# A 64 KB write of zeros beside the first loads, on a batched matmul that keeps its DMA engines full

## Chip, cores and metric

One core of a Trainium2 chip. The time is the device time of one execution in microseconds (us). A program on one core has no second die to compare with, so the state of a run (fast or slow) is judged against the fastest run of the same kernel.

## The reference

```python
batch, m, k, n = 16, 512, 768, 1024
x: (batch, k, m) float32,  y: (batch, k, n) float32
out = np.einsum('bkm,bkn->bmn', x, y)      # (batch, m, n) float32
```

Each batch reads 1.57 MB of x and 3.15 MB of y and writes 2.10 MB: 109 MB in all.

## The kernel before

SyncE issues everything that moves: per batch the load of x, the load of y, and the store of the batch four back (`LAG`). VectorE casts both to bf16, PE multiplies, ScalarE copies the sums out of PSUM. The last four stores, that of the last batch among them, follow after the loop. In the views PE stands for TensorE's matmuls, PEld for its weight loads, DVE for VectorE, ACT for ScalarE and POOL for GpSimd.

```python
    LAG = 4
    o_tiles = {}

    def store(b):
        nc.sync.dma_start(o_v[b], o_tiles.pop(b)[:])

    with tc.manual_schedule():
        for b in range(B):
            xs = xs_pool.tile([P, KT, M], FP32, name="xs")      # 2 buffers
            ys = ys_pool.tile([P, KT, N], FP32, name="ys")      # 2 buffers
            nc.sync.dma_start(xs[:], x_v[b])
            nc.sync.dma_start(ys[:], y_v[b])
            if b >= LAG:
                store(b - LAG)
            # ... casts on VectorE, 48 matmuls, 8 copies on ScalarE into o_sb (5 buffers) ...
            o_tiles[b] = o_sb
        for b in sorted(o_tiles):
            store(b)
```

Of the kernel before, what the change touches and what calls it, by code (L numbers as in the profile page):

```python
# [1 line left out]

_os.environ.setdefault("NEURON_RT_ULTRASERVER_MODE", "4")

# [1 line left out]

# [4 lines left out]


@with_exitstack
def kernel(
    ctx: ExitStack,
    tc: tile.TileContext,
    x: bass.AP,
    y: bass.AP,
    out: bass.AP,
):  # L20
    nc = tc.nc
    P = 128
    FP32 = mybir.dt.float32
    BF16 = mybir.dt.bfloat16

    B, K, M = x.shape
    _, _, N = y.shape
    KT = K // P
    MT = M // P
    NF = 512  # L30
    NT = N // NF



    x_v = x.rearrange("b (p ko) m -> b p ko m", ko=KT)
    y_v = y.rearrange("b (p ko) n -> b p ko n", ko=KT)
    o_v = out.rearrange("b (p mo) n -> b p mo n", mo=MT)

    xs_pool = ctx.enter_context(tc.tile_pool(name="xs_pool", bufs=2))
    ys_pool = ctx.enter_context(tc.tile_pool(name="ys_pool", bufs=2))  # L40
    x_pool = ctx.enter_context(tc.tile_pool(name="x_pool", bufs=2))
    y_pool = ctx.enter_context(tc.tile_pool(name="y_pool", bufs=2))
    o_pool = ctx.enter_context(tc.tile_pool(name="o_pool", bufs=5))
    psum = ctx.enter_context(tc.tile_pool(name="psum", bufs=8, space=bass.MemoryType.PSUM))
    LAG = 4

    o_tiles = {}

    def store(b):
        nc.sync.dma_start(o_v[b], o_tiles.pop(b)[:])  # L50

    with tc.manual_schedule():
        for b in range(B):
            xs = xs_pool.tile([P, KT, M], FP32, name="xs")
            ys = ys_pool.tile([P, KT, N], FP32, name="ys")
            nc.sync.dma_start(xs[:], x_v[b])  # L56
            nc.sync.dma_start(ys[:], y_v[b])  # L57
            if b >= LAG:
                store(b - LAG)
            x_sb = x_pool.tile([P, KT, M], BF16, name="x_sb")  # L60
            y_sb = y_pool.tile([P, KT, N], BF16, name="y_sb")
            nc.vector.tensor_copy(x_sb[:], xs[:])  # L62
            for h in range(2):
                ks = slice(h * KT // 2, (h + 1) * KT // 2)
                nc.vector.tensor_copy(y_sb[:, ks], ys[:, ks])  # L65
            x_w = x_sb[:].rearrange("p k (j mo) -> p k mo j", mo=MT)
            o_sb = o_pool.tile([P, MT, N], FP32, name="o_sb")
            o_tiles[b] = o_sb
            for mo in range(MT):
                for nt in range(NT):  # L70
                    ns = slice(nt * NF, (nt + 1) * NF)
                    ps = psum.tile([P, NF], FP32, name="ps")
                    for kt in range(KT):
                        nc.tensor.matmul(ps[:], x_w[:, kt, mo], y_sb[:, kt, ns],  # L74
                                         start=(kt == 0), stop=(kt == KT - 1))
                    nc.scalar.copy(o_sb[:, mo, ns], ps[:])  # L76
            if False:
                store(b)
        for b in sorted(o_tiles):
            store(b)  # L80


# [1 line left out]
_INS = ['x', 'y']  # L84
_OUTS = [((16, 512, 1024), 'float32')]


# [23 lines left out]
```

## Time and profile before

| | before |
|---|---|
| median of 6 runs (lowest to highest) | 261.97 us (261.90 to 262.24) |
| bytes moved, mean rate | 109.18 MB, 420 GB/s |
| DMA engines busy in slices 1 to 38 (of 40, counted from 0) | 90% or more |
| PE, VectorE, ScalarE busy | 74%, 32%, 29% |
| last y landed, to the end of the span | 235.0 us, 25.0 us more |

Read it from the DMA row: every slice but the first and the last is full, so only bytes, or time that the DMA engines lose, can move the end. The lines for this are shown in the prediction below.

### The profile page before, as it was taken

The numbers are of one execution on the slowest core, as the hardware profiler recorded it, in microseconds if no ns is written. First come the engines' busy times: TensorE is split into PE (matmuls) and PEld (weight loads), VectorE is DVE, ScalarE is ACT, GpSimd is POOL, SyncE is SP. The second block draws the span as 40 slices with busy tenths as digits, with TensorE's granted clock in tenths as the row PEclk, the third lists the DMA queues.
The fourth block names the chain that finished last, engine by engine and source line by source line (L and its number), as shares of the span: only waits on it lengthen the run. The fifth ranks groups of instructions, "written<-read, shape, count | busy, mean of one in ns | idle before, by whom it ended". The sixth has DMA issues, their size and how long they took to land.

```text
span 260.1 us, 1877 instructions
## 1 busy us (share of the span) xinstructions
PE 192.3 (74%) x768; PEld 89.3 (34%) x768; DVE 83.0 (32%) x48; ACT 76.4 (29%) x129; POOL 0.2 (0%) x4
## 2 busy tenths in 40 slices
PE   0059999896947939599597886939779395895950
PEld 0014555353523514235143342514334142351420
DVE  0271643525213252222524215252132522225000
ACT  1003444342421403314123241413324042141330
POOL 0000000000000000000000000000000000000000
PEclk9999999999997998959779797997999899796895
DMA  7999999999999999999999999999999999999995
GB/s 299 427 423 420 438 433 427 431 369 422 430 430 432 432 430 435 430 432 423 433 435 421 438 422 438 429 427 437 435 424 424 432 431 430 437 425 432 431 408 242
DMA packets 6921, 109.18 MB, mean 420 GB/s; under 512 B 768, under 2 KB 768, under 8 KB 768
## 3 DMA queue, kind: packets, MB, share of 16 engines
q1 hardware_dynamic: 6912, 109.05, 98.5%
q8 instruction: 6, 0.10, 0.1%
q14 instruction: 3, 0.02, 0.0%
HBM read 75.50 MB, written 33.55 MB: 419 GB/s over the span
## 4 chain that ended last, share of the span: by engine, by line
DMA 80%; DVE 10%; PE 5%; DVEq 1%; SPq 0%; issue 0%; ACT 0%
DMA ys<-in_y_dram 80%; DVE y_sb L65 10%; PE ps L74 5%; DVEq L106 1%; SPq L56 0%; ACT o_sb L76 0%; SPq L57 0%; DVEq L65 0%
## 5 line engine op out<-in xcount | busy, mean ns | idle before, releaser
L74 PE MATMUL ps<-y_sb,x_sb 128*128 128x512 bf16 x768 | 192.3, 413 | 58.4 <-DVE y_sb L65 58.4
L74 PEld LDWEIGHTS <-x_sb 128*128 128x128 bf16 x768 | 89.3, 118 | 160.9 <-issue 47.5
L76 ACT COPY o_sb<-ps 128x512 f32<-128x512 f32 x128 | 75.2, 587 | 174.1 <-PE ps L74 174.1
L65 DVE CAST y_sb<-ys 128x3072 bf16<-128x3072 f32 x32 | 54.9, 1757 | 89.4 <-DMA ys<-in_y_dram 89.4
L62 DVE CAST x_sb<-xs 128x3072 bf16<-128x3072 f32 x16 | 28.2, 1760 | 66.2 <-DMA xs<-in_x_dram 55.2
L76 ACT ACT_TABLE_LOAD x1 | 1.3, 1283 | 0.7 <-PEq L95 0.7
L95 POOL MEMSET const-uint8-127<- 128x1 uint8 x1 | 0.1, 103 | 0.0
L95 POOL MEMSET const-bfloat16-1.0<- 128x1 bf16 x1 | 0.1, 102 | 0.0
L95 POOL MEMSET const-float32-1.0<- 128x1 f32 x1 | 0.1, 100 | 0.0
L95 POOL MEMSET const-float32-0.0<- 128x1 f32 x1 | 0.1, 99 | 0.2 <-issue 0.2
## 6 DMA issues: line engine op xcount, KB each, us to landing
ys<-in_y_dram SPq DMA_DIRECT2D x16, 3072.0 KB, 28.1
out_dram<-o_sb SPq DMA_DIRECT2D x16, 2048.0 KB, 32.6
xs<-in_x_dram SPq DMA_DIRECT2D x16, 1536.0 KB, 29.7
```

Source lines behind the costliest of these rows:

```text
L62: nc.vector.tensor_copy(x_sb[:], xs[:])
L65: nc.vector.tensor_copy(y_sb[:, ks], ys[:, ks])
L74: nc.tensor.matmul(ps[:], x_w[:, kt, mo], y_sb[:, kt, ns], start=(kt == 0), stop=(kt == KT - 1))
L76: nc.scalar.copy(o_sb[:, mo, ns], ps[:])
L95: nc = _bacc.Bacc("TRN2", target_bir_lowering=False, num_devices=1)
L106: with _tile.TileContext(nc) as tc:
```

## The change

The intent: write something early to the output, so that whatever a first write costs falls where the loads are only starting, and not into the full stream. The rest of the diff rewrites the loops for a number of halves that is 1 here; the instructions on every engine, but for the two new ones (a memset on VectorE, a DMA issue on ScalarE), stay the same in the same order.

```diff
+        z_pool = ctx.enter_context(tc.tile_pool(name="z_pool", bufs=1))
+        z = z_pool.tile([P, 128], FP32, name="z")
+        nc.vector.memset(z[:], 0.0)
+        nc.scalar.dma_start(o_v[B - 1, :, 0, 0:128], z[:])
+
         for b in range(B):
             xs = xs_pool.tile([P, KT, M], FP32, name="xs")
             ys = ys_pool.tile([P, KT, N], FP32, name="ys")
-            nc.sync.dma_start(xs[:], x_v[b])
-            nc.sync.dma_start(ys[:], y_v[b])
+            halves = 1
+
+            load(xs[:], x_v[b], 1)
+            # ... cut: load of y in one half, matmul loop over one half: same instructions, same order
```

More of the change, by code (lines that the diff above doesn't have):

```diff
@@ L45, with load, mm @@
     LAG = 4
+    KH = KT // 2
     o_tiles = {}
+    def load(dst, src, rows):
+        nc.sync.dma_start(dst, src)
     def store(b):
         nc.sync.dma_start(o_v[b], o_tiles.pop(b)[:])
+    def mm(ps, x_w, y_sb, kt, mo, nt):
+        nc.tensor.matmul(ps[:], x_w[:, kt, mo], y_sb[:, kt, nt * NF:(nt + 1) * NF],
+                         start=(kt == 0), stop=(kt == KT - 1))
     with tc.manual_schedule():
+        z_pool = ctx.enter_context(tc.tile_pool(name="z_pool", bufs=1))
+        z = z_pool.tile([P, 128], FP32, name="z")
+        nc.vector.memset(z[:], 0.0)
+        nc.scalar.dma_start(o_v[B - 1, :, 0, 0:128], z[:])
         for b in range(B):
@@ L55 @@
             ys = ys_pool.tile([P, KT, N], FP32, name="ys")
-            nc.sync.dma_start(xs[:], x_v[b])
-            nc.sync.dma_start(ys[:], y_v[b])
+            halves = 1
+            load(xs[:], x_v[b], 1)
+            for h in range(halves):
+                ks = slice(h * KT // halves, (h + 1) * KT // halves)
+                load(ys[:, ks], y_v[b, :, ks], 1)
             if b >= LAG:
@@ L63 @@
             for h in range(2):
-                ks = slice(h * KT // 2, (h + 1) * KT // 2)
+                ks = slice(h * KH, (h + 1) * KH)
                 nc.vector.tensor_copy(y_sb[:, ks], ys[:, ks])
@@ L68 @@
             o_tiles[b] = o_sb
-            for mo in range(MT):
-                for nt in range(NT):
-                    ns = slice(nt * NF, (nt + 1) * NF)
-                    ps = psum.tile([P, NF], FP32, name="ps")
-                    for kt in range(KT):
-                        nc.tensor.matmul(ps[:], x_w[:, kt, mo], y_sb[:, kt, ns],
-                                         start=(kt == 0), stop=(kt == KT - 1))
-                    nc.scalar.copy(o_sb[:, mo, ns], ps[:])
-            if False:
-                store(b)
+            ps = {}
+            for h in range(halves):
+                for mo in range(MT):
+                    for nt in range(NT):
+                        if h == 0:
+                            ps[mo, nt] = psum.tile([P, NF], FP32, name="ps")
+                        for kt in range(h * KT // halves, (h + 1) * KT // halves):
+                            mm(ps[mo, nt], x_w, y_sb, kt, mo, nt)
+                        if h == halves - 1:
+                            nc.scalar.copy(o_sb[:, mo, nt * NF:(nt + 1) * NF], ps[mo, nt][:])
         for b in sorted(o_tiles):
```

## The prediction

> **What bounds the kernel now.** I read the page first: the chain that ended last, then the slices, then the waits, then the stretches in which the slices dip.
>
> ```profile
> DMA ys<-in_y_dram 80%; DVE y_sb L65 10%; PE ps L74 5%; DVEq L106 1%; SPq L56 0%; ACT o_sb L76 0%; SPq L57 0%; DVEq L65 0%
> DMA  7999999999999999999999999999999999999995
> GB/s 299 427 423 420 438 433 427 431 369 422 430 430 432 432 430 435 430 432 423 433 435 421 438 422 438 429 427 437 435 424 424 432 431 430 437 425 432 431 408 242
> q1 hardware_dynamic: 6912, 109.05, 98.5%
> ```
>
> The reader is to see three things. The chain is 80% loads of y. The 16 DMA engines are at 90% or more in every slice but the first and the last, and one queue (q1, SyncE's) carries nearly all of it. PE has 74% and all other engines less than 35%. So the kernel moves 109 MB at about 430 GB/s; time changes if bytes change or if the engines lose time. In the slices I look for lost time: slice 0 (start), slice 8 (369 where its neighbours have 430), slices 38 and 39 (end).
>
> The y load takes 28.1 us from issue to landing in the page's table of issues, while 3 MB at 430 GB/s are 7.3 us. So four to five transfers stand in the queue at any moment: a transfer that is issued later or earlier by a microsecond changes nothing, and a microsecond lost by all DMA engines is lost at the end.
>
> Slice 8 covers 52.0 to 58.5 us. In single microseconds (stretch, busy time of PE, PEld, DVE, ACT, POOL, granted clock, DMA share, GB/s):
>
> ```profile
> 54.00:55.00 1.00, 1.00 (x7) 0.51 (x5) 0.00 (x0) 0.59 (x1) 0.00 (x0) 1.00 0.97 418
> 55.00:56.00 1.00, 1.00 (x6) 0.52 (x5) 0.00 (x0) 0.59 (x1) 0.00 (x0) 1.00 1.26 393
> 56.00:57.00 1.00, 1.00 (x6) 0.56 (x5) 0.00 (x0) 0.34 (x1) 0.00 (x0) 1.00 0.79 221
> 57.00:58.00 1.00, 1.00 (x7) 0.49 (x6) 0.00 (x0) 0.29 (x2) 0.00 (x0) 1.00 1.03 311
> 58.00:59.00 1.00, 1.00 (x6) 0.54 (x5) 0.00 (x0) 0.54 (x1) 0.00 (x0) 1.00 0.73 311
> 59.00:60.00 1.00, 1.00 (x6) 0.54 (x5) 0.00 (x0) 0.59 (x1) 0.00 (x0) 1.00 0.97 418
> ```
>
> From 55 to 59 us the core moved 1236 KB in place of 4 x 430 = 1720: 484 KB short, 1.1 us of the engines' time. No other stretch between 3 and 250 us dips like this. What happens there? In SyncE's part of the timeline, the first store of the program is issued behind the y load of batch 4:
>
> ```profile
> 39.71 0.33 SPq L57 DMA_DIRECT2D ys<-in_y_dram  x1
> 40.09 0.42 SPq L50 DMA_DIRECT2D out_dram<-o_sb  x1
> ```
>
> Ahead of it in the queue are five batches of loads, 5 x 4.72 MB = 23.6 MB, which at 425 GB/s are 55.5 us after the first packet at 1.7 us: the first store reaches the engines at about 57 us. The trace's packet records agree: its first packet starts at 57.74 us, and the last one or two y packets of each DMA engine before it took 1.3 to 1.96 us where a y packet takes 0.91. The excess, summed over 54 to 58 us and divided by 16, is 0.92 us per engine. The later stores show none: between 60 and 250 us the excess stays under 0.06 us in every 10 us. So the first write of the program, or the first on this queue, costs each engine 0.92 us, once, at the price of reads that stand ahead of it. That is what the change can act on.
>
> The end (same columns):
>
> ```profile
> 250.00:251.00 1.00, 0.67 (x4) 0.11 (x1) 0.00 (x0) 0.29 (x2) 0.00 (x0) 1.00 0.88 377
> 251.00:252.00 1.00, 0.00 (x0) 0.00 (x0) 0.00 (x0) 0.29 (x1) 0.00 (x0) 1.00 0.66 279
> 252.00:253.00 1.00, 0.00 (x0) 0.00 (x0) 0.00 (x0) 0.00 (x0) 0.00 (x0) 1.00 1.19 508
> ```
>
> The last y lands at 235.0 us, batch 15's matmuls and copies end at 251.3, and its store follows. The engines have by then nearly drained stores 11 to 14 (four times 2.1 MB, 19.5 us at 430): only around 251.5 us are some of them free. Both paths start from the landing of the last y, so a saving or a loss before it moves the whole end with it, one for one.
>
> **What the Trainium skill says.** "DMA: Bandwidth & Descriptors", section "Issuing engines are not separate DMA queues": transfers from SyncE and ScalarE run on the same 16 DMA engines and interleave; another issuing engine saves only issue time. Here issue is 0.33 to 0.42 us and hidden, so ScalarE's queue brings no bandwidth; the trace of before has only one queue in use and can't show the interleaving. The section "Queues, rings and completion order" of that page: each DMA engine goes round-robin between queues, packet by packet. So the zeros don't wait behind 9 MB of loads as they would on SyncE's queue, but go between two packets of the first load. "Rules for kernel authors" there: transfers under 64 KB pay mostly overhead. The section "Latency and other measured facts" names 0.6 us to the first byte; here the first load is issued at 0.73 us and its first packet starts at 1.74, so 1.0 us. No page that I found states a cost of a first write; the 0.92 us is this trace's alone.
>
> **The change part by part.**
> - VectorE: one more memset, 128x128 f32. The casts take 1757 ns for 3072 elements, 0.57 ns each, so 128 elements are about 0.07 us and a fixed part near the 0.1 us of GpSimd's tiny memsets: estimate 0.15 us, at about 0.7 us, where VectorE is idle until 6.90. On no path.
> - ScalarE: one more issue of about 0.4 us, at about 1 us, ahead of the table load of 1.28 us. The first copy is at 19.2 us. On no path.
> - DMA: 64 KB more. By bandwidth 65.5 KB / 430 = 0.15 us; as 128 packets of 512 B, 8 for each engine, an estimate of 20 to 30 ns each (32 times fewer bytes than the 611 ns packet of a store, 19 ns, and a little overhead), 0.2 us. It stands in front of the bound: plus 0.2 us.
> - Waits: I compared the instruction order. Matmuls, casts, copies and SyncE's transfers come in the same order and number; the loops over halves have one half, so the rest of the diff changes nothing. The semaphores that transfers share in turn shift by one, and the x load of batch 4 waits in addition for the zeros, done some 25 us earlier. So the last store can't overtake them, and nothing waits.
> - The first-write cost: 0.92 us at 57 us. If it is paid once by whichever write comes first, it goes to about 2 us. There the first x packets are slow anyway: the 16 or so first ones took 0.55 to 1.2 us where 0.46 is usual (excess per engine 0.44 us), and the engines are only starting. So between nothing and all of it is hidden there.
>
> Sum: 261.97 + 0.2 - (0 to 0.92) = 261.25 to 262.2.
>
> **The rivals.**
> 1. The cost goes to the start and hides beside the start-up of the loads: 261.97 + 0.2 - 0.9 = 261.3. For it: the dip is tied to the first store, never comes back, and the start has latency to hide it in. Against: the engines are kept full from 3 us on.
> 2. The cost goes to the start but is paid in full, since what stalls is a DMA engine, and a stall of loads at 2 us counts like one at 57: 262.2. For it: at 57 us it was reads ahead of the write that were held up, so x packets may be held up too.
> 3. The cost belongs to SyncE's queue, or to each region of the output, or to the engines' first turn from long reading to writing: the zeros on ScalarE's queue then cure nothing, the dip stays at 57 us: 262.2.
> 4. Something larger, such as a second queue that disturbs the engines for long. It has 128 packets and is empty afterwards; nothing speaks for it.
>
> I give 1 (in part or whole) about 50%, 2 and 3 together 45%.
>
> **Range and chances.** The middle between 261.3 and 262.2, weighed toward a partial saving, is 261.6. The repeats of before spread by 0.2 us, and another build may have another end by a few tenths (the granted clock differs in the last stages). Range 260.9 to 262.5. Two per cent are 5.2 us; the largest cost that I found and the change could touch is 0.92. So "within 2%" is nearly certain: 0.98.
>
> **What would show it.** In the changed kernel's slices, slice 8 should come up from 369 to about 430 if the cost moved (1 or 2), and stay if it is rival 3. The single microseconds from 1 to 5 tell 1 from 2: the first x load landed at 6.9 us; near 7.1 is rival 1, near 8 rival 2. The last y should land at 235.0 plus what the total moves by, and the time from there to the end should stay 25.0 us. The prediction is wrong if the last y lands at another distance from the end, if the bandwidth outside slices 0 and 8 changes, or if a copy, cast or matmul waits for the zeros.

## The result, and the profile after

262.25 us median of 6 runs (262.03 to 263.04) against 261.97: ratio 1.0012, 95% interval 0.9998 to 1.0025. (A ratio is the mean time of one kernel's fast runs over that of the other's of the same rounds, so not quite the ratio of the medians quoted.) Nothing clear of noise happened.

The page of the changed kernel, the rate in the 40 slices and the queues (packets, MB, share of 16 engines):

```profile
GB/s 274 446 430 410 440 425 445 423 367 425 438 429 433 426 426 440 424 440 416 437 432 421 440 418 439 429 423 444 424 433 427 420 442 428 437 423 432 420 428 221
q1 hardware_dynamic: 6912, 109.05, 98.4%
q10 hardware_dynamic: 144, 0.07, 0.1%
```

Slice 8 is at 367, before it was 369. The dip that the early write could have cured is still there. The zeros are the new queue q10: 128 packets of data and 16 that signal their end.

In single microseconds (stretch, busy time of PE, PEld, DVE, ACT, POOL, granted clock, DMA share, GB/s), to be laid beside the six lines in the prediction:

```profile
54.00:55.00 1.00, 1.00 (x7) 0.49 (x6) 0.00 (x0) 0.59 (x1) 0.00 (x0) 1.00 1.15 492
55.00:56.00 1.00, 1.00 (x6) 0.56 (x5) 0.00 (x0) 0.59 (x1) 0.00 (x0) 1.00 1.24 418
56.00:57.00 1.00, 1.00 (x7) 0.52 (x5) 0.00 (x0) 0.29 (x1) 0.00 (x0) 1.00 0.85 270
57.00:58.00 1.00, 1.00 (x6) 0.50 (x5) 0.00 (x0) 0.29 (x1) 0.00 (x0) 1.00 0.96 270
58.00:59.00 1.00, 1.00 (x6) 0.57 (x5) 0.00 (x0) 0.59 (x1) 0.00 (x0) 1.00 0.69 295
59.00:60.00 1.00, 1.00 (x7) 0.49 (x5) 0.00 (x0) 0.59 (x1) 0.00 (x0) 1.00 1.09 467
```

From 55 to 59 us 1253 KB moved, before 1236. The packet records tell it the same way: y packets that start at 55 to 60 us carry 0.82 us of excess per engine here, 0.92 before.

The start, from the timeline (start, duration, engine, line, operation), and the issue row of the zeros (KB, us from issue to landing):

```profile
0.73 0.38 SPq L50 DMA_DIRECT2D xs<-in_x_dram  x1
0.82 0.17 DVE L63 MEMSET z<- 128x128 f32 x1 [0.82 <-PEq L115]
1.02 0.41 ACTq L64 DMA_DIRECT2D out_dram<-z  x1
...
7.38 1.76 DVE L80 CAST x_sb<-xs 128x3072 bf16<-128x3072 f32 x1 [6.39 <-DMA xs<-in_x_dram]
```

```profile
out_dram<-z ACTq DMA_DIRECT2D x1, 64.0 KB, 11.0
```

Two readings. First, the zeros needed 11.0 us to land. In the packet records their first packet starts at 4.98 us, four microseconds after the issue, and the last of data at 10.75; each takes 27 ns, and each engine puts one between two packets of its loads. Second, the first cast starts at 7.38 us where it was 6.90. It is tempting to charge this to the zeros. The first experiment shows that one must not.

The last y landed at 235.35 us (235.03 before), and from there to the end it is 25.1 us (25.0 before). As the prediction had it, the end moved with the last y.

### The profile page after: what moved, and what is told of

It is laid out like the page before. It is cut to its first block, busy times and chain, and to the rows that moved or that the text cites. A ratio compares the mean times of both kernels' runs of the same rounds, so it can differ in the third digit from the quotient of the medians.

```text
span 260.5 us, 1879 instructions
## 1 busy us (share of the span) xinstructions
PE 191.4 (73%) x768; PEld 89.2 (34%) x768; DVE 83.2 (32%) x49; ACT 76.4 (29%) x129; POOL 0.2 (0%) x4
## 4 chain that ended last, share of the span: by engine, by line
DMA 80%; DVE 10%; PE 4%; DVEq 1%; SPq 0%; issue 0%; ACT 0%
DMA ys<-in_y_dram 80%; DVE y_sb L83 10%; PE ps L56 4%; DVEq L126 1%; SPq L50 0%; ACT o_sb L98 0%; DVEq L83 0%
```

## The experiments

All results were correct. The kernel before ran beside each group: its median was 262.01 us beside e1 to e4, 261.95 beside e5 to e8 and 262.12 beside e9 to e12. Two measures are used on every trace: the rate in four microseconds that end 0.1 to 1.3 us after the first store's first packet (430 GB/s is the undisturbed rate), and the excess per engine, the time by which y packets there exceed 0.914 us, summed and divided by 16. The excess comes from the packet records in the trace, which no view prints; all runs have it in a table after e8. It is the better measure: a view counts a packet where it starts, so a rate hangs on where its window lies (e2 and e3 show by how much).

### e1: the zeros taken out, all else as changed

```diff
-        z_pool = ctx.enter_context(tc.tile_pool(name="z_pool", bufs=1))
-        z = z_pool.tile([P, 128], FP32, name="z")
-        nc.vector.memset(z[:], 0.0)
-        nc.scalar.dma_start(o_v[B - 1, :, 0, 0:128], z[:])
```

> The changed kernel without the block of zeros, all else as changed (undo of the one part that does anything). If the zeros are the whole of the 0.3 us between the two kernels, this one is at the time of the kernel before: 261.97, ratio 1.000 within 0.001, first x load landed at about 6.9 us. If the refactoring of the loops costs something after all, it stays near 262.25, ratio 1.001.

Measured: 261.95 us (5 runs), ratio 0.9997 (0.9985 to 1.001). So no cost of the rewritten loops shows; the interval reaches from 0.4 us less to 0.3 us more. But its timeline has

```profile
7.40 1.76 DVE L76 CAST x_sb<-xs 128x3072 bf16<-128x3072 f32 x1 [7.40 <-DMA xs<-in_x_dram]
```

without any zeros: the expected 6.9 us was wrong. The start differs by half a microsecond from profile to profile of kernels with the same transfers in the same order, so the late first load of the changed kernel isn't an effect of the change. The stretch of the dip differs too:

```profile
55.00:59.00 4.00, 4.00 (x21) 2.10 (x19) 0.00 (x0) 1.87 (x4) 0.00 (x0) 1.00 1.00 363
```

363 GB/s are 0.62 us lost ((430 - 363) / 430 x 4) and an excess of 0.61, where the profiles of before and after gave 1.1 and 0.8 to 0.9. From here on this profile is the comparison, since it comes from the same chip job as the next three.

### e2: the zeros on SyncE's queue, and e3: the zeros to the first batch's output

```diff
-        nc.scalar.dma_start(o_v[B - 1, :, 0, 0:128], z[:])
+        nc.sync.dma_start(o_v[B - 1, :, 0, 0:128], z[:])        # e2
+        nc.scalar.dma_start(o_v[0, :, 0, 0:128], z[:])          # e3
```

> The same 64 KB of zeros, but on SyncE's queue, ahead of the first x load. Theory A (the lost 0.9 us at 55 to 59 us belong to the first write of this queue): the dip is gone, stretch 55 to 59 us moves about 1720 KB in place of 1250, time about 261.3 or, if the cost is paid in full at the start, 262.2. Theory B (they belong to the region of the output that is written first) and theory C (to the first long run of writes behind reads, however often something small was written before): the dip stays, 1250 KB, and the time is 262.2 to 262.5, the zeros and their wait for the memset ahead of the first load being on the path (0.3 to 0.5 us).

> Zeros on ScalarE's queue as in the change, but written to the first batch's output, which is what the first real store writes. Theory B (first touch of that region): the dip at 55 to 59 us is gone or at least halved, time about 261.4. Theories A and C: the dip stays at 1250 KB, time 262.25.

Measured: e2 262.43 us (5 runs), ratio 1.0017 (1.0004 to 1.0029); e3 262.18 us (4 runs), ratio 1.0005 (0.9991 to 1.0018). The stretch of the dip in e2:

```profile
55.00:59.00 4.00, 4.00 (x20) 2.05 (x19) 0.39 (x1) 1.76 (x3) 0.00 (x0) 1.00 0.94 352
```

and in e3:

```profile
55.00:59.00 4.00, 4.00 (x21) 2.05 (x19) 0.00 (x0) 1.88 (x4) 0.00 (x0) 1.00 0.96 350
```

These stand beside e1's 363, but half a microsecond later e1's own window gives

```profile
55.50:59.50 4.00, 4.00 (x20) 2.14 (x19) 0.00 (x0) 1.76 (x3) 0.00 (x0) 1.00 0.87 313
```

so the rates cannot rank the three. The excess is 0.47 us in e2, 0.58 in e3 and 0.61 in e1: the cost stays. That speaks against this queue's first write (A) and against the region that is written first (B), with a loophole: 64 KB may be too small to count as a first write of either. e5 and e10 close it. There zeros on ScalarE's queue, to the last batch's output, free the first store on SyncE's queue, to the first batch's output, of its dip. On SyncE's queue the zeros' first packet comes 0.86 us after their issue, and the first x packet at 2.47 us in place of 1.73: there the zeros do delay the loads, which fits the slightly longer time.

### e4: no zeros, stores one batch earlier

```diff
-    LAG = 4
+    LAG = 3
```

> No zeros, and every store is queued one batch earlier (lag 3 in place of 4), so the first store stands behind four batches of loads, 18.9 MB, and its packets start near 46.5 us. If the dip belongs to the first store, whatever the cause (A, B, C), it moves to about 44 to 48 us, 0.9 us per engine again, and 55 to 59 us is at 1720 KB. If it belongs to the time or to the count of transfers in the queue, it stays at 55 to 59 us. Time within 1 us of before.

Measured in two stretches, the dip's new place and its old one:

```profile
44.00:48.00 4.00, 4.00 (x20) 2.06 (x19) 0.00 (x0) 1.76 (x3) 0.00 (x0) 1.00 0.96 326
55.00:59.00 4.00, 4.00 (x21) 2.09 (x19) 0.55 (x1) 1.76 (x3) 0.00 (x0) 1.00 1.05 452
```

The dip goes with the first store. It isn't a matter of the time, nor of the first instruction fetch, which is at 38.1 us here and at 37.6 us before. The expected time was a miss: 264.84 us (4 runs, 262.88 to 265.24), ratio 1.0088. One more store stands ahead of the last y, which lands at 239.99 us instead of 235.03, and one store fewer is left to fill the engines during the last 48 matmuls:

```profile
253.00:256.00 3.00, 2.12 (x10) 0.91 (x8) 0.00 (x0) 1.32 (x3) 0.00 (x0) 1.00 0.03 11
```

### e5: a whole 2 MB of zeros, early

```diff
-        z = z_pool.tile([P, 128], FP32, name="z")
-        nc.scalar.dma_start(o_v[B - 1, :, 0, 0:128], z[:])
+        z = z_pool.tile([P, MT, N], FP32, name="z")
+        nc.scalar.dma_start(o_v[B - 1], z[:])
```

> A whole 2 MB of zeros to the last batch's output on ScalarE's queue at the start. Theory T (the dip at the first real store is a cost of the first large write, paid once): no dip at the first real store, which now reaches the engines near 62 us; the cost appears in the first 25 us. Theory S (the dip comes from all 16 engines turning from reads to the first store at the same moment, while later turns are spread over about 3 us): the dip at the first real store stays, some 0.6 to 1.1 us of lost transfer. Time in either case about 261.97 + 4.9 us (2.1 MB at 430 GB/s) = 266.9; under T about 266.3.

Measured: 266.83 us (4 runs), ratio 1.0189. The zeros' packets of 16 KB start at 9.12 us, the first real store's at 62.7:

```profile
9.00:10.00 1.00, 0.00 (x0) 0.11 (x1) 0.19 (x1) 0.00 (x0) 0.00 (x0) 1.00 0.79 287
10.00:13.00 3.00, 0.00 (x0) 0.00 (x0) 0.00 (x0) 0.00 (x0) 0.00 (x0) 1.00 0.98 421
59.00:63.00 4.00, 3.95 (x20) 2.10 (x19) 0.98 (x1) 1.88 (x4) 0.00 (x0) 1.00 1.01 434
```

Now the dip at the real store is gone (434 GB/s, excess 0.01 us), and loads pay 0.76 us of excess at 5 to 10 us, most of it ahead of the zeros' first packet, as at the first store of the other runs. So a large early write does take the cost, and nothing is won by it: the kernel is 4.9 us slower than the one before, which is the time of the zeros' bytes. The total agrees with the sum without a saving, 266.9, not with 266.3 (the interval of the ratio, 1.0175 to 1.0203, is 4.6 to 5.3 us more).

### e6: eight times the zeros in packets of 512 B

```diff
-        z = z_pool.tile([P, 128], FP32, name="z")
-        nc.scalar.dma_start(o_v[B - 1, :, 0, 0:128], z[:])
+        z = z_pool.tile([P, 8, 128], FP32, name="z")
+        nc.scalar.dma_start(o_v[B - 1].rearrange("p mo (h n) -> p (mo h) n", h=2)[:, :, 0:128], z[:])
```

> Eight times the zeros (512 KB) as 1024 packets of 512 B in one transfer on ScalarE's queue. A packet of zeros took 27 ns in the changed kernel's trace and 64 fall to each engine: 1.73 us, so 263.7 if the cost is the packets' time. If it is bytes at 430 GB/s: 1.22 us, 263.2. If the 0.3 us of the change were a fixed cost of a second queue or noise, it stays at 262.2.

Measured: 268.24 us (5 runs), ratio 1.0242 (1.0228 to 1.0256): 6.3 us, not 1.7. The waits of SyncE (us in total, times, longest) name it:

```profile
SPq L50 <- DMA out_dram<-z: 19.8, 1, 19.8
```

```profile
48.00:50.00 2.00, 2.00 (x11) 1.02 (x9) 0.23 (x1) 0.79 (x2) 0.00 (x0) 1.00 0.04 16
60.00:64.00 4.00, 3.12 (x15) 1.41 (x13) 0.00 (x0) 1.76 (x3) 0.00 (x0) 1.00 0.97 285
```

Transfers take turns on eight semaphores, and the instruction order shows the x load of batch 4 waiting for the zeros, with which it shares one. 64 small packets for each engine, one between every two load packets, last until 49 us. That load is due at 31 us, so SyncE stands 19.8 us and the engines run dry at 48 to 50 us. From 47 to 54 us they move 1274 KB in place of 3010, which is 4.0 of the 6.3 us. The prediction's "done some 25 us earlier" was 19 us with 8 packets (they landed at 12.0 us, the load was issued at 31.33); 64 use it all up. And a clue: the excess at the first store, 1.23 us here, is larger than in any run whose engines did not run dry. No large write came before it, so e6 does not say whether a cost already paid comes back.

### e7: no zeros, the queue drained once in mid-program

```diff
+    def drain(t):      # waits until the store that reads t has landed; later loads queue behind
+        nc.sync.dma_start(t[:, 0, 0:128], x_v[0, :, 0, 0:128])
             if b >= LAG:
+                t = o_tiles[b - LAG]
                 store(b - LAG)
+                if b == 8:
+                    drain(t)
```

> No zeros; in batch 8 a small load waits until the store before it has landed, so the queue runs empty once near 130 us and all engines start again at the same time; x and y of batch 9 and then store 5 follow, as at the first store. Theory S: a second dip of 0.6 to 1.1 us just ahead of store 5's first packets, with y packets of 1.2 to 1.9 us in place of 0.91. Theory T (a first time, once): no y packet there is slowed, no dip other than the drain itself. The time is 3 to 6 us longer by the drain under both.

Measured (one run, its time not used): before the first store and before store 5, whose first packet is at 143.6 us,

```profile
54.00:58.00 4.00, 4.00 (x20) 2.12 (x19) 0.08 (x1) 1.76 (x3) 0.00 (x0) 1.00 1.03 373
120.00:124.00 4.00, 2.74 (x13) 1.24 (x11) 0.00 (x0) 1.76 (x3) 0.00 (x0) 1.00 0.95 408
140.00:144.00 4.00, 0.00 (x0) 0.00 (x0) 0.00 (x0) 0.00 (x0) 0.00 (x0) 1.00 0.90 236
```

The middle line is an ordinary stretch ahead of a later store, for comparison. No packet starts between 128.8 and 130.1 us: the engines are empty. After that the dip comes back, and larger: 30 of the 33 y packets that start at 140 to 144 us take 1.35 to 2.06 us, and the excess is 1.39 us per engine (0.67 at this run's first store). So it is not a cost that a program pays once (T). The theory that fits e7 was S, that all engines turn to the store at the same moment. e5 speaks against S, but there one engine was behind the others by 2 us when the real store came (in the kernel before, which has the dip, one was 2.9 us behind too). So both were tried again with lag 2, where no instruction fetch has come between.

### e9 and e10: lag 2, without and with the 2 MB of zeros

```diff
-    LAG = 4
+    LAG = 2          # e9 without zeros; e10 with the zeros of e5
```

> No zeros, lag 2: the first store stands behind three batches of loads and reaches the engines near 35 to 36 us, before the first instruction fetch sets one engine back, so all 16 engines turn from reads to it within about 1 us. All theories of a cost at the first large store expect the dip there, 0.6 to 1.1 us. The time is long, since two stores fewer are left for the end: near 270 us; it is not the point. Control for the next run.

> Lag 2 with the whole 2 MB of zeros on ScalarE's queue at the start. Theory S (all engines turn at the same moment): y packets just ahead of the first real store (near 40 us) are slowed again, 0.6 us or more per engine, since the engines end y within 1 us of each other. Theory I (a large write after the engines began from rest, at the start or after the queue ran empty, costs once; while transfers go on it is not paid again): none there, under 0.1 us, and about 0.8 us in the first 25 us as in the run with lag 4.

Measured ahead of the first real store, e9 (its first packet at 35.95 us):

```profile
33.00:37.00 4.00, 4.00 (x20) 2.06 (x19) 0.00 (x0) 1.81 (x4) 0.00 (x0) 1.00 0.98 315
```

and e10 (zeros from 9.2 us, first real store at 40.84 us):

```profile
7.00:11.00 4.00, 0.00 (x0) 0.11 (x1) 1.76 (x1) 0.00 (x0) 0.00 (x0) 1.00 0.96 340
37.00:41.00 4.00, 4.00 (x21) 2.09 (x19) 0.00 (x0) 1.88 (x4) 0.00 (x0) 1.00 1.02 438
```

In e10 the 16 engines end the last y ahead of the store within 0.91 us of each other, in phase, and there is no excess at all; in e9 it is 0.97 us. The zeros' own place, 5 to 10 us, has 0.69 us. S falls. Theory I is left: the first large write after the engines have started from rest costs each of them 0.4 to 1.4 us of slowed loads, once, and again after they have run empty. That it comes back rests on one profile, e7.

### e11 and e12: the cost of the zeros by themselves

```diff
-        z = z_pool.tile([P, 128], FP32, name="z")
+        z = z_pool.tile([P, MT, 128], FP32, name="z")   # e11, to o_v[B - 1, :, :, 0:128]
+        z = z_pool.tile([P, N], FP32, name="z")         # e12, to o_v[B - 1, :, 0, :]
```

> Four times the zeros as 512 packets of 512 B on ScalarE's queue. In the run with eight times as many they took one turn for each packet of the loads, landed 47.9 us after their issue, and SyncE stood still 19.8 us because the x load of batch 4 waits for them; the queue ran empty. Here they should land near 27 us, before that load is due at 31 us. Then the cost is 32 packets x 27 ns = 0.86 us per engine over the kernel without zeros: 262.8, ratio 1.003. If the wait bites here too: 264 or more.

> 512 KB of zeros as 128 packets of 4 KB: the bytes of the run with eight times the zeros, but only 8 packets for each engine. They land by about 12 us as in the change, nobody waits for them, and they cost their bytes: 524 KB at 430 GB/s = 1.2 us, 263.2, ratio 1.005. If 512 KB of early writes are enough to count as the first large write, the dip at the first real store is gone; if a large packet or more bytes are needed, it stays.

Measured: e11 262.69 us (5 runs), ratio 1.0019 (1.0006 to 1.0033), beside 262.12 of the kernel before: 0.57 us by the medians for 256 KB, or 0.14 for each 64 KB. The zeros landed 26.1 us after the issue and SyncE did not wait for them. e12 263.31 us (4 runs), ratio 1.0041 (1.0028 to 1.0055): 1.2 us for 512 KB, as expected from bytes. Both fit the bytes at 430 GB/s (0.61 and 1.22 us); e11's 27 ns for each packet, 0.86 us, is within its interval too (it spans 0.16 to 0.86 us), so packets or bytes is not decided by it. In e12 the dip at the first store is at

```profile
55.00:59.00 4.00, 4.00 (x20) 2.08 (x19) 0.63 (x1) 1.83 (x4) 0.00 (x0) 1.00 0.96 367
```

and the excess is 0.44 us: 512 KB in packets of 4 KB do not take the cost away as 2 MB do. In e11 it is 0.65 us.

### e8: no zeros, stores one batch later

```diff
-    LAG = 4
-    o_pool = ctx.enter_context(tc.tile_pool(name="o_pool", bufs=5))
+    LAG = 5
+    o_pool = ctx.enter_context(tc.tile_pool(name="o_pool", bufs=6))
```

> No zeros; every store one batch later (lag 5, six output buffers). Lag 3 cost 2.8 us since too few stores were left to fill the engines during the last batch's matmuls. In the kernel before, the engines are partly idle only around 251 to 252 us, some 0.3 us. Lag 5 should fill that: 261.6 to 261.8, ratio 0.999. If something else sets the end: 262.0. The dip should move to about 66 to 69 us with the first store.

Measured: 261.68 us (5 runs, 261.63 to 261.75) beside 261.95 for the kernel before, ratio 0.9992 (0.998 to 1.0005). The median is where it was expected, but the interval includes 1, so a gain over before isn't shown. The dip moved along to 65 to 69 us:

```profile
65.00:69.00 4.00, 4.00 (x20) 2.13 (x19) 0.26 (x1) 1.76 (x3) 0.00 (x0) 1.00 0.95 350
```

### The excess at the first store, all runs

Excess per engine in us, over y packets that start from 4 us before to 1 us after the first store's first packet:

| zeros ahead of it | excess |
|---|---|
| none | before 0.92, e1 0.61, e4 0.80, e7 0.67, e8 0.51, e9 0.97 |
| 64 to 512 KB | after 0.82, e2 0.47, e3 0.58, e11 0.65, e12 0.44 |
| 512 KB, engines then ran dry | e6 1.23 |
| 2 MB | e5 0.01, e10 0.00 |

The 2 MB cure it, clear of all scatter. The means of the first two rows, 0.75 and 0.59, differ by less than the spread within either, so a partial cure by small writes is neither shown nor excluded.

## Why the prediction was right, and where its steps were not

Time and class were right: 262.25 lies in 260.9 to 262.5, and "within 2%" holds. The range held because it was wide enough for the rivals as well; the mechanism that the prediction favoured did not occur. By its steps:

- **The bound.** Right. From 59 to 235 us both kernels move 430 GB/s, and the end followed the last y.
- **The cost of the zeros, plus 0.2 us.** Fits, within the noise. Four times the zeros gave 0.57 us, 0.14 for each 64 KB; the change itself gave 0.28 by the medians, with an interval of its ratio that includes 1.
- **The packets, 20 to 30 ns each.** Right: 27 ns.
- **The place of the zeros.** Wrong, without harm. They were to go "between two packets of the first load", near 2 us. They started at 4.98 us and went on until 10.8, one between every two load packets.
- **Waits.** Right for 64 KB, and e6 shows how close such a wait lies: it is the shared semaphore, not the data, that ties the loads to the zeros.
- **The first-write cost goes to about 2 us and is partly hidden (rival 1, given 50%).** This is the step that failed, and it put the point at 261.6 and not at 262.2. The cost did not move: the excess at the first store is 0.82 us in the changed kernel and 0.92 before, within the scatter. The sign that was to tell rivals 1 and 2 apart, the landing of the first x load (7.1 or 8 us), told nothing: it was 7.4 us with the zeros and without (e1). Rival 3 was right in its result, 262.2. Of its three reasons e2, e3 and above all e5 and e10 refute the queue and the region. The third, the first turn to writing, is nearest, but "first" has to be read as the first large write since the engines were at rest: a large write moves the cost (e5, e10), a drain renews it (e7 alone), small writes do not move it (e2, e3, e11, e12). Rival 2's thought, that a moved cost is paid in full at the start, is what e5 shows, to within its 0.3 us.

What stays open is the mechanism: what in the engines or the memory makes the last two or three loads ahead of that write take up to 2 us in place of 0.91. Also where between 512 KB in packets of 4 KB and 2 MB in packets of 16 KB the limit lies, and whether bytes or packet size decide. And the dip's size scatters between profiles, 0.4 to 0.9 us per engine among kernels with lag 4 and 5 whose engines did not run dry, so one profile does not show a difference of half of it.

## What to carry to other kernels

When the DMA engines are full, ask of an early or dummy transfer only two things: its bytes at the stream's rate, and who will wait for its semaphore. Before a half microsecond in one profile is called an effect, run the program without the change's active part on the same chip: here that control had the same late start. Here the one-time cost was moved only by a write of 2 MB, whose own bytes took 4.9 us, and moving it saved nothing.

## What the Trainium skill lacked or had wrong

- "DMA: Bandwidth & Descriptors", section "Latency and other measured facts", gives about 0.6 us to the first byte on this path. On SyncE's queue the zeros' first packet came 0.86 us after the issue began (e2), the first load's 1.0 us (before); but on ScalarE's queue, beside bulk loads on SyncE's, 3.9 to 4.2 us in all seven traces that have zeros there, also where the last of these loads had been issued 3.1 us before (e5). The page has no figure for this delay.
- The same page, section "Queues, rings and completion order", says that each engine turns between queues packet by packet, and the trace of after agrees: the zeros lie singly between load packets. It lacks what follows in time: beside packets of 12 to 24 KB, 8 packets of 512 B per engine took until 10.8 us, 32 until 26.7 and 64 until 49.2, so that a small transfer lands late in proportion to its packets. The 64 packets made a later load that shared their semaphore wait 19.8 us (e6).
- The same page, "Rules for kernel authors", says that transfers under 64 KB pay mostly overhead. No run here has one so small. What the page does not tell apart is the transfer's own time and its cost to a full stream: 64 KB took 11.0 us to land and moved the kernel by 0.28 us, within the noise; 256 KB in 512 B packets took 26.1 and cost 0.57.
- No page that I found has the cost of the first large write after rest: 0.4 to 1.0 us for each engine at the first store, 1.39 us after a drain (one profile).
